# A sixth raw buffer, other planning numbers, and constants for the last bank's bits, in a two-layer hybrid attention kernel

## The chip, the cores and the metric

The kernel runs on one core of a Trainium2 chip. The metric is the time on the device in microseconds (us). Engines: PE (TensorE, matmuls; PEld its weight loads), DVE (VectorE), ACT (ScalarE), POOL (GpSimd), SP (which issues most DMAs).

## What is computed

Two layers over x (256 tokens, 1024 wide) and a memory mem of 256 tokens; `depth` is 2, heads are 64 wide.

```python
h = rms_norm(x, norm_g[layer]);  proj = h @ w_in[layer]          # 1024 x 3584
sb_q, sb_k, sb_v, sb_g, mb_q, mb_k, mb_v, mb_g, mem_q, mem_g = split(proj)
o_sb  = stick_breaking_attention(sb_q, sb_k, sb_v) * silu(sb_g)   # 6 heads
o_mb  = moba_attention(rope(mb_q), rope(mb_k), mb_v) * silu(mb_g) # 6 heads; here plain causal softmax
mk, mv = split(rms_norm(mem, mem_norm_g[layer]) @ w_mem_kv[layer])
o_mem = softmax_attention(mem_q, mk, mv) * silu(mem_g)            # 4 heads
x = x + concat(o_sb, o_mb, o_mem) @ w_out[layer]
# behind the last layer: rms_norm(x, final_norm_g)
```

Stick-breaking weights are exp(log sigmoid(z) + the sum over later keys of log(1 - sigmoid)).

## The kernel before

Every weight matrix is a **piece** (sb_qk, mb_q, mk, mv, ..., wo0 to wo2 for the output projection), loaded in **chunks** of 128 rows by 768 f32 values (384 KB) into a ring of `RAW` tiles, raw. ACT or DVE rounds a chunk to its **high part** (a cast, line 265 or 286) and DVE computes the **low part**, raw minus high (line 271); both lie in hl, a ring of seven. A product is three matmuls: high by high, high by low, low by high (the activations are split in the same way, into the tiles T, or mxhi and mxlo). The load of chunk j + RAW is issued by SP when the low part of chunk j has been queued:

```python
dma(raws[j % RAW]..., p.src[...], ("raw", j), q, now)      # dma_chunk
tt(los[j % LEAD], raws[j % RAW], his[j % LEAD], OP.subtract); dma_chunk(S.cur.t)   # lo_task
```

Nothing is ordered by hand beyond the lists `ORDER` (pieces by layer) and `KORD` (in which order the output projection takes its eight rows of 128). While the program is built, a list scheduler (`Sched`) plays all tasks against estimated engine times, DMA rates (`DMA_GBS`, `DMA_LAT`, ...), priorities (`PRI`, `P_*`) and slacks, and picks what each engine does next; the outcome is one fixed sequence for each engine, and on the chip each engine works its own off in order. So a number that only the scheduler reads changes the time through the sequence alone.

What the names in the rows are. Layer 0 works on h without the row factor of the norm; that factor, rbx, goes from DVE through a POOL DMA to DRAM and back to all partitions, and sb_q, sb_k and mem_q are multiplied by it on DVE. Score matmuls and value matmuls of a pair of heads use half the rows or columns of PE (`pair_scores`, form "row"; `pair_task`, form "col"); `HOLD` and `CROWD` say how long such a pair is held back to be bundled with others. For the softmax heads the weights are turned by a **trip**: DVE transposes 32-blocks into D, SP stores D to DRAM (Z) and loads it back turned in four DMAs (T<-Z; for rope ga or uT). The names in `HALVES` get eight DMAs instead. junk is a scratch tile: PE warms up on it, and ACT writes the squares of its row statistics there. In the last layer the last bank of wo2 is started by a matmul of no use, which sets the bank's bits (later it is overwritten by a copy of the residual, and the products accumulate on that).

Of the kernel before, what the change touches and what calls it, by code (L numbers as in the profile page):

```python
# [8 lines left out]
FR = mybir.dt.float32r  # L9
# [15 lines left out]
        "mb_q": (1536, 384), "mb_k": (1920, 384), "mb_v": (2304, 384), "mb_g": (2688, 384),  # L25
        "mem_q": (3072, 256), "mem_g": (3328, 256)}
LEAD = 7
RAW = 5
KORD = ((4, 5, 2, 3, 0, 1, 6, 7), (4, 5, 0, 1, 2, 3, 6, 7))
LAT_SAME, LAT_CROSS = 130.0, 240.0  # L30
PE_LATE = 173.4
NORM_LATE = 1845.2
DG_LATE = 816.9
COLD = 3900.0
PRI = {"sb": (54, 36), "mb": (6, 40), "mem": (44, 48)}
P_EV = 26
P_H0 = -8
P_RX = 2
P_M0 = 42
P_RM = 47  # L40
P_M1 = 50
URG = 2
X_AT = {5: 4, 6: 5, 7: 6, 8: 7}
CST_AT = 11
X0_AT = 9
X1_AT = 15
DMA_GBS = 355.0
SP_ISSUE = 450.0
POOL_ISSUE = 1000.0
POOL_TRIP = 5000.0  # L50
DMA_LAT = 2200.0
DMA_GBS_1K = 300.0
TRIP_LAT = 3500.0
MEM_AT = 1
ORDER = (["sb_qk", "mb_q", "mb_k", "mk", "mem_q", "mv", "sb_g", "sb_v", "mb_g", "mb_v", "mem_g"],
         ["mk", "mv", "mb_q", "mb_k", "sb_k", "sb_g", "mem_q", "sb_q", "sb_v", "mb_g", "mb_v", "mem_g"])
GATES = {"sb_g": ((0, 1), (2,)), "mb_g": ((0, 1), (2,)), "mem_g": ((0,), (1,))}
HOLD = 2000.0
HALVES = []
CROWD = 1  # L60
SPARE1 = 4
SPARE2 = 1
DVE_HI = 800.5
SLACK_PE = 26.0
SLACK = 104.7


def _free(ap):
    n = 1
    for d in ap.shape[1:]:  # L70
        n *= d
    return n
# [18 lines left out]
class Sched:  # L91
# [37 lines left out]
    def _avail(self, k, eng):  # L129
# [82 lines left out]
def hybrid_trunk(ctx: ExitStack, tc: tile.TileContext, x, mem, norm_g, w_in, w_mem_kv, w_out,  # L212
# [5 lines left out]
    S = Sched()  # L218
# [20 lines left out]
    def mm(out, lhsT, rhs, start, stop, **kw):  # L239
        n = _free(rhs)  # L240
        half = lhsT.shape[0] == 64 or out.shape[0] == 64
        if lhsT.dtype == FR:
            c = max(111.0, n * 0.4167 + (20.0 if n > 384 else 13.0))
        elif lhsT.dtype == BF:
            c = max(28.0, n * 0.44)
        else:
            c = max(110.0, n * 1.667 + 10.0)
        nc.tensor.matmul(out, lhsT=lhsT, rhs=rhs, start=start, stop=stop, **kw)  # L248
        m = (lhsT.shape[0], out.shape[0])
        c = (0.5 * c if half else c) + pe_mode(m, lhsT.dtype)  # L250
        S.op("pe", c * (1.8 if S.T["pe"] < COLD else 1.0))
# [41 lines left out]
    def sb(name, shape, dt=F32):  # L293
        return cpool.tile(shape, dt, name=name)
# [4 lines left out]
    gc = sb("gc", [128, 32])  # L299
    smask = sb("smask", [128, 128])  # L300
    cmask = sb("cmask", [128, 256])
    negT = sb("negT", [128, 128], FR)
    negone = sb("negone", [128, 128], FR)
    junk = sb("junk", [128, 512], BF)
    gb = sb("gb", [128, D])
    uT = sb("uT", [128, KT, 256])
# [14 lines left out]
    S.res["a"] = Res([sb(f"a{i}", [128, 384]) for i in range(3)])  # L321
    S.res["w"] = Res([sb(f"w{i}", [128, 512]) for i in range(4)])
    S.res["ah"] = Res([(sb(f"ah{i}", [128, 384], FR), sb(f"al{i}", [128, 384], FR)) for i in range(2)])
    S.res["wT"] = Res([sb(f"wT{i}", [128, 384]) for i in range(5)])
    S.res["D"] = Res([sb(f"D{i}", [128, 1024]) for i in range(2)])
    S.res["F0"], S.res["F1"] = Res([]), Res([])
    dpool = ctx.enter_context(tc.tile_pool(name="turn", bufs=1, space=bass.MemoryType.DRAM))
# [16 lines left out]
    dma_t = {"t": 500.0}  # L344

    def queue(nbytes, run, now):

        dma_t["t"] = max(dma_t["t"], now) + nbytes / (400.0 if run >= 3072 else DMA_GBS if run > 1024 else DMA_GBS_1K)
        return dma_t["t"] + DMA_LAT

    def dma(dst, src, name=None, q=None, now=0.0):
# [39 lines left out]
    for p in order:  # L391
        i = 0
# [13 lines left out]
    def dma_chunk(now=0.0, q=None):  # L406
        j = prog["dma"]
        if j >= len(chunks):
            return
        p, kk, c, w = chunks[j]  # L410
        n = len(kk)
        dma(raws[j % RAW][:, :n * w].rearrange("p (k c) -> p k c", c=w),
            p.src[:, kk[0]:kk[0] + n, c:c + w], ("raw", j), q, now)
        prog["dma"] += 1
        if j in X_AT:
            load_xT(X_AT[j], X_AT[j] + 1, now=now)
        for t, at in enumerate((X0_AT, X1_AT)):
            if j == at:
                dma(xs[:, t, :], x_r[:, t, :], ("x", t), now=now)
        if j == CST_AT:  # L420
            dma(cst, consts[:, 0:512], "cst", now=now)
            dma(S.res["w"].items[0][2][:, :256], consts[:, 512:768], "msk", now=now)

    def hi_task():
        for j, (p, kk, _, w) in enumerate(chunks):
            w = len(kk) * w
            e, _ = yield R(*([] if j in (0, 2) else [("act", 0.833 * w)]), ("dve", 0.52 * w + DVE_HI), 
                           need=[("raw", j)] + ([("free", j - LEAD)] if j >= LEAD else []))
            copy(his[j % LEAD][:, :w], raws[j % RAW][:, :w], e)
# [32 lines left out]
    load_xT(2, 3)  # L462
    dma_chunk()
    load_xT(3, 4)

    def bcast_row(vec, name):
        nc.gpsimd.dma_start(gb, bass.AP(tensor=vec.tensor, offset=vec.offset, ap=[[0, 128], [1, D]]))
        S.ready[name] = S.cur.t + 4000.0

    def setup():  # L470
        yield R("pool")
# [104 lines left out]
    def rows_done(key, name, rb):  # L576
        z = dpool.tile([1, 256], F32, name="rows_" + key)
        yield R("dve", need=["setup0", (key, "rows", 0), (key, "rows", 1)])
        nc.vector.transpose(rt, rcx if key == "x" else rcm)
        S.op("dve", 100.0)  # L580
        yield R("pool")
        for t in range(2):
            nc.gpsimd.dma_start(z[:, t * 128:t * 128 + 128].rearrange("o (i a) -> (o i) a", i=4), rt[t:128:32, :])
        S.op("pool", 2.0 * POOL_ISSUE)
        S.ready[name, "dump"] = S.cur.t + POOL_TRIP
        yield R("pool", need=[(name, "dump")])
        nc.gpsimd.dma_start(rb, z.broadcast_to([128, 256]))
        S.op("pool", POOL_ISSUE)
        S.ready[name] = S.cur.t + POOL_TRIP

    def rows_task(l, src, key, name, rc, rb):
        for t in range(2):
# [3 lines left out]
    def norm_task(l, t, H, done):  # L596
# [423 lines left out]
    def main():  # L1020
# [26 lines left out]
        for l in range(DEPTH):  # L1047
# [15 lines left out]
            def T_piece(n, X, nchunk, need, post):  # L1063
                p = pieces[n, l]
                for c in range(nchunk):
                    acc = yield from bank()
                    yield from tr_unit(p, X, c, acc, need, c == nchunk - 1)
                    S.spawn(post(c, acc), P_EV, S.cur.t)

            def N_piece(n, X, need, post):  # L1070
                p = pieces[n, l]
                for t in range(2):
                    acc = yield from bank()
                    yield from nat_unit(p, X, t, acc if n == "mv" else acc[:, :p.width], need)
                    S.spawn(post(t, acc), P_EV, S.cur.t)

# [5 lines left out]
            for h in range(SBH):  # L1082
                S.spawn(sb_head(l, h), PRI["sb"][1] + h)
            for h in range(MEMH):
                S.spawn(soft_head(l, h, "mem"), PRI["mem"][1] + h)
            for h in range(SBH):
                S.spawn(soft_head(l, h, "mb"), PRI["mb"][1] + h)
            for kind, n in (("sb", 3), ("mb", 3), ("mem", 2)):
                for c in range(n):
                    S.spawn(pair_scores(l, kind, c), PRI[kind][0] + 2)  # L1090
                    S.spawn(pair_sums(l, c) if kind == "sb" else pair_turn(l, kind, c), PRI[kind][0] + 1)
                    S.spawn(pair_task(l, kind, c), PRI[kind][0])
            if l == 0:
                p = pieces["sb_qk", 0]
                accs = []
# [70 lines left out]
            accs = {}  # L1166
            for i, k0, k1 in ((0, 0, 6), (1, 0, 6), (0, 6, 8), (1, 6, 8), (2, 0, 8)):
                p = pieces[f"wo{i}", l]
                w = p.width
                for t in range(2):  # L1170
                    if k0 == 0 and (i, t) not in accs:
                        accs[i, t] = yield from bank()
                    if (l, i, t) == (1, 2, 0):
                        accs[2, 1] = yield from bank()
                        mm(accs[2, 1][:, :256], junk[:, :128], junk[:, :256], True, True)
                        S.spawn(seed_task(accs[2, 1]), 0, S.cur.t)
                    yield from nat_unit(p, X, t, accs[i, t][:, :w], xneed, k0, k1, (l, i, t) == (1, 2, 1))
                    if k1 == KT:
                        S.spawn(resid_task(l, i, t, accs[i, t], w, hN), 0, S.cur.t)
# [58 lines left out]
```

## Time and profile before

| | |
|---|---|
| three timed runs | 275.11, 278.11, 277.42 us; median 277.42 |
| the profiled execution | 277.1 us, of which the span of the instructions is 275.2 |
| busy | PE 96%, PEld 87%, DVE 83%, ACT 70%, POOL 3% of the span |
| granted PE clock | 0.994 |
| moved | 62.34 MB, 226 GB/s |
| chain that ended last | PE 84%, DVE 9%, DMA 2%, ACT 1% |

A row of the timeline has the start, the length, the engine, the line, the operation, out<-in, shape and count; in brackets the idle time before it and what ended it. Neighbouring instructions of a kind are merged, and since matmuls are pipelined the distance of two starts says more than a length.

### The profile page before, as it was taken

To read this page: it belongs to the slowest core of one execution; us is meant where nothing else is said; L and a number is where in the kernel's file an instruction comes from. 1 tells how busy PE (TensorE), PEld (TensorE's weight loads), DVE (VectorE), ACT (ScalarE), POOL (GpSimd) and SP (SyncE) were. 2 spreads that over 40 slices of the span, in tenths; PEclk is the share of its full clock that TensorE was granted. 3 is DMA by queue.
4 is the path that set the end of the run, shared out by engine and by line. 5 is a ranking of instruction groups with operands and counts; after the bars stand their busy time and mean duration, and the time that the engine had idled before them with its cause. 6 is when DMAs were issued, how large, how long until landed. Compare 5 with 4: busy or idle time off the path is not lost.

```text
span 275.2 us, 4955 instructions
## 1 busy us (share of the span) xinstructions
PE 265.4 (96%) x1653; PEld 239.1 (87%) x1653; DVE 229.6 (83%) x543; ACT 193.0 (70%) x441; POOL 7.6 (3%) x19
## 2 busy tenths in 40 slices
PE   8999997999999999999999999999999999999992
PEld 5889995897997898898988999888889889898991
DVE  3797996999999999995889778649999999979082
ACT  3787994998888596770886545559699689675053
POOL 0002100002000000000000000000000000000000
PEclk9999999999999999999999999999999999999997
DMA  6999989986977789684487866777348876972004
GB/s 213 338 399 369 347 237 316 296 260 180 296 229 210 231 259 272 232 200 152 132 248 250 288 225 225 232 225 204 89 163 245 260 242 182 341 231 88 0 2 152
DMA packets 47593, 62.34 MB, mean 226 GB/s; under 512 B 3728, under 2 KB 44048, under 8 KB 47568
## 3 DMA queue, kind: packets, MB, share of 16 engines
q1 hardware_dynamic: 46480, 59.93, 69.1%
q0 software_dynamic: 512, 1.31, 1.7%
q10 hardware_dynamic: 576, 0.79, 0.8%
q8 instruction: 13, 0.21, 0.3%
q14 instruction: 12, 0.10, 0.1%
HBM read 54.94 MB, written 7.08 MB: 225 GB/s over the span
## 4 chain that ended last, share of the span: by engine, by line
PE 84%; DVE 9%; DMA 2%; issue 1%; ACT 1%; DVEq 0%
PE bank L248 84%; DVE hl L271 3%; DMA raw<-in_w_mem_kv_dram 2%; DVE al L271 1%; DVE bank L271 1%; PE bank L254 1%; DVE xs L271 1%; DVE mem_q L275 0%; ACT junk L267 0%; ACT hl L265 0%; DVE a L275 0%; DVE ah L286 0%; DVE sb_k L275 0%; DVE sb_q L275 0%; DVE mv L275 0%
## 5 line engine op out<-in xcount | busy, mean ns | idle before, releaser
L271 DVE TENSOR_TENSOR hl<-raw,hl 128x768 fp32r<-128x768 f32 (+3 forms) x114 | 101.4, 899 | 11.7 <-ACT hl L265 10.5
L248 PE MATMUL bank<-T,hl 128*128 128x512 f32 (+1 forms) x582 | 107.1, 340 | 0.6 <-DVE st L740 0.6
L248 PEld LDWEIGHTS bank<-T,hl 128*128 128x128 f32 x582 | 89.2, 190 | 14.6 <-issue 1.7
L265 ACT CAST hl<-raw 128x768 fp32r<-128x768 f32 (+2 forms) x111 | 87.4, 796 | 15.2 <-PE bank L248 4.4
L248 PE MATMUL bank<-hl,T 128*128 128x384 f32 (+1 forms) x448 | 80.3, 336 | 0.0
L248 PEld LDWEIGHTS bank<-hl,T 128*128 128x128 f32 x448 | 76.7, 188 | 1.8 <-issue 0.3
L248 PE MATMUL bank<-hl,mxhi 128*128 128x384 f32 (+1 forms) x192 | 45.2, 319 | 0.0
L248 PEld LDWEIGHTS bank<-hl,mxhi 128*128 128x128 f32 x192 | 33.3, 189 | 0.8 <-issue 0.8
L248 PE MATMUL bank<-hl,mxlo 128*128 128x384 f32 (+1 forms) x96 | 30.4, 317 | 0.0
L267 ACT ACTIVATE junk<-xs 128x384 bf16<-128x384 f32 (+2 forms) x15 | 8.0, 537 | 20.8 <-DVE xs L271 20.3
L248 PEld LDWEIGHTS bank<-hl,mxlo 128*128 128x128 f32 x96 | 18.1, 189 | 0.1
L267 ACT ACTIVATE ga<-ga 128x256 f32<-128x256 f32 (+1 forms) x36 | 17.4, 488 | 0.9 <-DVE ga L275 0.7
L267 ACT ACTIVATE T<-uT,gc 128x256 fp32r<-128x256 f32 x24 | 11.8, 502 | 3.9 <-DMA uT<-xT_dram 3.9
L265 ACT COPY gT<-bank 128x256 f32<-128x256 f32 x16 | 5.9, 370 | 11.6 <-PE bank L248 11.4
L271 DVE TENSOR_TENSOR xs<-bank,xs 128x384 f32<-128x384 f32 (+1 forms) x11 | 5.7, 520 | 8.7 <-PE bank L248 8.7
L267 ACT ACTIVATE a<-a 128x384 f32<-128x384 f32 x24 | 12.4, 533 | 0.0
L783 DVE STREAM_TRANSPOSE D<-w 128x384 f32<-128x384 f32 (+1 forms) x20 | 12.4, 623 | 0.0
L275 DVE SCALAR_TENSOR_TENSOR T<-uT,gc,T 128x256 fp32r<-128x256 f32 x24 | 11.4, 480 | 1.1 <-ACT T L267 1.1
L279 DVE TENSOR_SCALAR w<-w,st 128x256 f32<-128x256 f32 (+1 forms) x40 | 11.3, 327 | 0.0
L267 ACT ACTIVATE w<-w,st 128x128 f32<-128x128 f32 (+1 forms) x24 | 10.6, 446 | 0.7 <-DVE st L740 0.5
L271 DVE TENSOR_TENSOR gT<-bank,gT 128x256 f32<-128x256 f32 x16 | 6.7, 417 | 4.1 <-ACT gT L265 4.1
L267 ACT ACTIVATE w<-bank,st 128x256 f32<-128x256 f32 x16 | 7.4, 474 | 2.4 <-DVE st L753 2.4
(114 smaller groups left out, 261.4 us busy)
## 6 DMA issues: line engine op xcount, KB each, us to landing
raw<-in_w_in_dram SPq DMA_DIRECT2D x70, 384.0 KB, 4.5
raw<-in_w_out_dram SPq DMA_DIRECT2D x17, 384.0 KB, 4.6
Z<-D SPq DMA_DIRECT2D x10, 384.0 KB, 4.2
raw<-in_w_mem_kv_dram SPq DMA_DIRECT2D x8, 384.0 KB, 5.4
T<-Z SPq DMA_DIRECT2D x24, 96.0 KB, 4.3
uT<-memT_dram SPq DMA_DIRECT2D x8, 256.0 KB, 6.5
Z<-D SPq DMA_DIRECT2D x4, 512.0 KB, 4.5
T<-Z SPq DMA_DIRECT2D x16, 128.0 KB, 4.8
```

The lines of the kernel that those rows point to most:

```text
L248: nc.tensor.matmul(out, lhsT=lhsT, rhs=rhs, start=start, stop=stop, **kw)
L254: nc.tensor.transpose(out, in_, idt)
L265: nc.scalar.copy(out, in_)
L267: nc.scalar.activation(out, in_, func, **kw)
L271: nc.vector.tensor_tensor(out, a, b, op=op)
L275: nc.vector.scalar_tensor_tensor(out, a, s, b, op0=op0, op1=op1)
L279: nc.vector.tensor_scalar(out, a, s, None, op0=op)
L783: nc.vector.transpose(o, w[:, :n * 128].rearrange("p (m j r) -> p m j r", j=4, r=32))
```

## The change

RAW goes from 5 to 6, with a load more ahead of the first instruction; to make room, the wT ring goes from 5 to 4 tiles. The scheduler's DMA rates are lower, and the two broadcasts of rows go through its queue model. Its priorities, slacks, ORDER, KORD, HOLD and SPARE2 have other values, and five trips are in HALVES. negT and negone become one tile, neg, and the matmul that sets the last bank's bits reads neg instead of junk.

```diff
-RAW = 5
-KORD = ((4, 5, 2, 3, 0, 1, 6, 7), (4, 5, 0, 1, 2, 3, 6, 7))
+RAW = 6
+KORD = ((0, 1, 2, 3, 4, 5, 6, 7), (2, 3, 0, 1, 4, 5, 6, 7))
...
-DMA_GBS = 355.0
+DMA_GBS = 330.0
...
-MEM_AT = 1
-ORDER = (["sb_qk", "mb_q", "mb_k", "mk", "mem_q", "mv", "sb_g", "sb_v", "mb_g", "mb_v", "mem_g"],
+MEM_AT = 0
+ORDER = (["sb_qk", "mb_q", "mb_k", "mem_q", "mv", "sb_g", "mk", "sb_v", "mb_v", "mb_g", "mem_g"],
...
-HOLD = 2000.0
-HALVES = []
+HOLD = 10878.7
+HALVES = [("F", 1, "mb", 1), ("F", 0, "mem", 1), ("F", 1, "mem", 1), ("F", 1, "mb", 2), ("F", 0, "mem", 0)]
...
-    negT = sb("negT", [128, 128], FR)
-    negone = sb("negone", [128, 128], FR)
+    neg = sb("neg", [128, 256], FR)
+    negT, negone = neg[:, 0:128], neg[:, 128:256]
...
-    S.res["wT"] = Res([sb(f"wT{i}", [128, 384]) for i in range(5)])
+    S.res["wT"] = Res([sb(f"wT{i}", [128, 384]) for i in range(4)])
...
+    for _ in range(RAW - 5):
+        dma_chunk()
...
-                        mm(accs[2, 1][:, :256], junk[:, :128], junk[:, :256], True, True)
+                        mm(accs[2, 1][:, :256], negone, neg, True, True)
```

What this makes of the sequences is shown at three places. First PE, layer 0, at the first scores of the stick-breaking heads (out sb_q, sb_k). Before, T_74 holds the tokens and T_75 the memory; in the change T_73 holds the tokens and T_74 the memory. Eight matmuls of mem_q stand between the last of mk and the scores before:

```order
L248 MATMUL bank_105<-T_75,hl_100 128x512
L248 MATMUL bank_106<-T_74,hl_94 128x512
L248 MATMUL bank_106<-T_74,hl_94 128x256
L248 MATMUL bank_106<-T_74,hl_94 128x512
L248 MATMUL bank_106<-T_74,hl_94 128x256
L248 MATMUL bank_106<-T_74,hl_94 128x512
L248 MATMUL bank_106<-T_74,hl_94 128x256
L248 MATMUL bank_106<-T_74,hl_95 128x512
L248 MATMUL bank_106<-T_74,hl_95 128x256
L248 MATMUL bank_108<-sb_q,sb_k 128x256
```

Now, with all of mem_q and nearly all of mv ahead of them (the last rows of the 60):

```order
L248 MATMUL bank_106<-hl_94,T_74 128x512
L248 MATMUL bank_106<-hl_94,T_74 128x256
L248 MATMUL bank_106<-hl_95,T_74 128x512
L248 MATMUL bank_106<-hl_95,T_74 128x256
L248 MATMUL bank_106<-hl_95,T_74 128x512
L248 MATMUL bank_106<-hl_95,T_74 128x256
L248 MATMUL bank_107<-sb_q,sb_k 128x256
```

The scores stand 20 matmuls later behind mb_k than they did. Second DVE at the same place, down to the products that the scores need. The rows hl<-raw are low parts. Before:

```order
L271 TENSOR_TENSOR rn_136<-rn_136,cst 128x6x16
L271 TENSOR_TENSOR rn_136<-rn_136,ru_137 128x6x16
L898 STREAM_TRANSPOSE D_126<-rn_136 128x3x4x32
L271 TENSOR_TENSOR hl_97<-raw_93,hl_97 128x768
L275 SCALAR_TENSOR_TENSOR mem_k<-bank_104,mem_k 128x256
L275 SCALAR_TENSOR_TENSOR sb_q<-sb_q,rbx 128x256 x3
L275 SCALAR_TENSOR_TENSOR sb_k<-sb_k,rbx 128x256 x3
```

Now:

```order
L901 STREAM_TRANSPOSE D_125<-rn_135 128x3x4x32
L271 TENSOR_TENSOR hl_96<-raw_93,hl_96 128x512
L271 TENSOR_TENSOR hl_97<-raw_88,hl_97 128x768
L275 SCALAR_TENSOR_TENSOR mem_q<-bank_108,mem_q 128x256
L271 TENSOR_TENSOR hl_98<-raw_89,hl_98 128x768
L551 TENSOR_SCALAR ss_157<-ss_157 128x1
L275 SCALAR_TENSOR_TENSOR sb_q<-sb_q,rbx 128x256 x3
L275 SCALAR_TENSOR_TENSOR sb_k<-sb_k,rbx 128x256 x3
```

hl_97 holds chunk 24 in both; it belongs to mv before and to sb_g now, and chunk 25 (hl_98) now stands ahead of sb_q too. Third SP, at the end of layer 0, where the trips of the memory heads (Z, then T) stand among the loads of the output projection. Before:

```order
L928 DMA T_75<-Z_131 32x4x256 x4
L352 DMA raw_89<-in_w_out_dram 128x2x384
L352 DMA raw_90<-in_w_out_dram 128x2x384
L917 DMA Z_129<-D_125 128x1024
L352 DMA raw_91<-in_w_out_dram 128x2x384
L352 DMA raw_92<-in_w_out_dram 128x2x384
L352 DMA raw_93<-in_w_out_dram 128x2x256
L352 DMA raw_89<-in_w_out_dram 128x2x256
L928 DMA T_75<-Z_129 32x4x256 x4
```

Now:

```order
L920 DMA Z_128<-D_124 128x1024
L352 DMA raw_91<-in_w_out_dram 128x2x384
L352 DMA raw_92<-in_w_out_dram 128x2x384
L931 DMA T_74<-Z_130 32x2x256 x8
L352 DMA raw_93<-in_w_out_dram 128x2x384
L352 DMA raw_88<-in_w_out_dram 128x3x256
L931 DMA T_74<-Z_128 32x2x256 x8
```

Both trips come back in eight smaller DMAs; two loads stand between the two trips' loads now, where two loads, a store and four loads stood.

More of the change, by code (lines that the diff above doesn't have):

```diff
@@ L27 @@
 LEAD = 7
-RAW = 5
-KORD = ((4, 5, 2, 3, 0, 1, 6, 7), (4, 5, 0, 1, 2, 3, 6, 7))
+RAW = 6
+KORD = ((0, 1, 2, 3, 4, 5, 6, 7), (2, 3, 0, 1, 4, 5, 6, 7))
 LAT_SAME, LAT_CROSS = 130.0, 240.0
-PE_LATE = 173.4
-NORM_LATE = 1845.2
-DG_LATE = 816.9
+PE_LATE = 303.1
+NORM_LATE = 361.3
+DG_LATE = 226.3
 COLD = 3900.0
-PRI = {"sb": (54, 36), "mb": (6, 40), "mem": (44, 48)}
-P_EV = 26
+PRI = {"sb": (58, 36), "mb": (18, 36), "mem": (48, 52)}
+P_EV = 23
 P_H0 = -8
[L38 to L41, printed above, removed]
+P_RX = -3
+P_M0 = 27
+P_RM = 37
+P_M1 = 60
 URG = 2
@@ L44 @@
 CST_AT = 11
-X0_AT = 9
+X0_AT = 11
 X1_AT = 15
-DMA_GBS = 355.0
+DMA_GBS = 330.0
 SP_ISSUE = 450.0
 POOL_ISSUE = 1000.0
-POOL_TRIP = 5000.0
+POOL_TRIP = 5500.0
 DMA_LAT = 2200.0
-DMA_GBS_1K = 300.0
+DMA_GBS_1K = 285.0
 TRIP_LAT = 3500.0
-MEM_AT = 1
-ORDER = (["sb_qk", "mb_q", "mb_k", "mk", "mem_q", "mv", "sb_g", "sb_v", "mb_g", "mb_v", "mem_g"],
-         ["mk", "mv", "mb_q", "mb_k", "sb_k", "sb_g", "mem_q", "sb_q", "sb_v", "mb_g", "mb_v", "mem_g"])
+MEM_AT = 0
+ORDER = (["sb_qk", "mb_q", "mb_k", "mem_q", "mv", "sb_g", "mk", "sb_v", "mb_v", "mb_g", "mem_g"],
+         ["mv", "mk", "mb_q", "mb_k", "sb_k", "sb_g", "mem_q", "sb_q", "sb_v", "mb_g", "mb_v", "mem_g"])
 GATES = {"sb_g": ((0, 1), (2,)), "mb_g": ((0, 1), (2,)), "mem_g": ((0,), (1,))}
-HOLD = 2000.0
-HALVES = []
+HOLD = 10878.7
+HALVES = [("F", 1, "mb", 1), ("F", 0, "mem", 1), ("F", 1, "mem", 1), ("F", 1, "mb", 2), ("F", 0, "mem", 0)]
 CROWD = 1
 SPARE1 = 4
[L62 to L65, printed above, removed]
+SPARE2 = 2
+DVE_HI = 647.3
+SLACK_PE = 0.0
+SLACK = 104.6
 def _free(ap):
@@ L346, in queue @@
     def queue(nbytes, run, now):
-        dma_t["t"] = max(dma_t["t"], now) + nbytes / (400.0 if run >= 3072 else DMA_GBS if run > 1024 else DMA_GBS_1K)
+        dma_t["t"] = max(dma_t["t"], now) + nbytes / (380.0 if run >= 3072 else DMA_GBS if run > 1024 else DMA_GBS_1K)
         return dma_t["t"] + DMA_LAT
@@ L464, in hybrid_trunk @@
     load_xT(3, 4)
+    for _ in range(RAW - 5):
+        dma_chunk()
     def bcast_row(vec, name):
         nc.gpsimd.dma_start(gb, bass.AP(tensor=vec.tensor, offset=vec.offset, ap=[[0, 128], [1, D]]))
-        S.ready[name] = S.cur.t + 4000.0
+        S.ready[name] = queue(524288, 4096, S.cur.t + 2400.0) + 1000.0
     def setup():
@@ L588, in rows_done @@
         S.op("pool", POOL_ISSUE)
-        S.ready[name] = S.cur.t + POOL_TRIP
+        queue(400000, 4096, S.cur.t)
+        S.ready[name] = S.cur.t + POOL_TRIP + 1500.0
     def rows_task(l, src, key, name, rc, rb):
```

## The prediction

> **What bounds the kernel now.** I read the busy table first, then the list of who waited for whom, then the timeline around the longest wait, then the stretches.
>
> ```profile
> PE 265.4 (96%) x1653; PEld 239.1 (87%) x1653; DVE 229.6 (83%) x543; ACT 193.0 (70%) x441; POOL 7.6 (3%) x19
> PE bank L248 <- DVE sb_k L275: 2.4, 1, 2.4
> PE bank L248 <- DVE junk L1023: 1.2, 1, 1.2
> PE bank L248 <- DVE st L740: 0.6, 1, 0.6
> PE bank L248 <- ACT junk L267: 0.3, 1, 0.3
> ```
>
> TensorE (PE) is busy for 96% of the span, and the four rows of waits are all it ever waits: 2.4 for the scaled sb_k, 0.6 for a softmax statistic, 0.3 for the scratch tile junk, and 1.2 at the start. Nothing else stands between its matmuls but the cost of changing their form. So this change can win what lies in three rows, 3.3 us and a little more, by removing waits; every other gain would need cheaper matmuls, and there the order is permuted, not shortened. Now the longest wait.
>
> ```profile
> 38.97 7.16 PE L248 MATMUL bank<-T,hl 128*128 128x512 f32 x40
> 48.49 2.23 PE L248 MATMUL bank<-sb_q,sb_k 64*128 64x256 f32 x24 [2.37 <-DVE sb_k L275]
> 38.34 1.02 SPq L352 DMA_DIRECT2D raw<-in_w_mem_kv_dram  x2
> 44.94 0.84 ACT L265 CAST hl<-raw 128x768 fp32r<-128x768 f32 x1 [4.18 <-DMA raw<-in_w_mem_kv_dram]
> 45.80 0.96 DVE L271 TENSOR_TENSOR hl<-raw,hl 128x768 fp32r<-128x768 f32 x1 [2.61 <-ACT hl L265]
> 47.10 1.00 DVE sb_q L275 x3
> 48.10 1.01 DVE sb_k L275 x3
> 54.97 2.63 PE L248 MATMUL bank<-hl,T 128*128 128x512 f32 x14
> ```
>
> Read backwards (columns: start, length, engine, line, what; in brackets the idle time before it and who ended it). The first score matmuls of the stick-breaking heads start at 48.49, after 2.37 of idling. They wait for sb_k, which DVE scales by rbx only after sb_q. DVE gets there late since, in its fixed order, it first computes the low part of a weight chunk of mv; that waits for ACT's high part, and that waits until 44.94 for the chunk, issued from 38.34 on: 6.6 us. The first matmul of mv stands at 54.97, ten us later (last row): the chunk is looked ahead for, and the engine that looks ahead is blocked.
>
> ```profile
> 48.50:120.80 72.30, 71.74 (x461) 63.23 (x462) 70.54 (x185) 60.87 (x148) 2.25 (x4) 1.00 0.82 245
> 132.40:260.00 127.60, 127.60 (x807) 116.13 (x806) 105.40 (x238) 86.62 (x192) 0.54 (x1) 1.00 0.67 209
> ```
>
> The stretches (busy PE, PEld, DVE, ACT, POOL, then clock, DMA share, GB/s): from the scores to wo1, the second piece of layer 0's output projection, PE has 71.74 of 72.30 and DVE 70.54, 97.6%: two engines bound this stretch. In layer 1 PE is full and DVE has 22 us to spare. The granted clock is 1.00 in both.
>
> **The scores of layer 0.** In the new order, between mb_k and the scores, stand the 32 matmuls of mem_q and 28 of mv, where 32 of mk and 8 of mem_q stood: 20 more. The first row quoted above has 40 matmuls from 38.97 to 46.13, 0.18 each; 20 take 3.5 to 3.6. PE then reaches the scores at 46.1 + 3.5 = 49.6 without waiting, later than sb_k was there even before (48.49). On DVE two low parts (chunks 24 and 25) and a piece of mem_q stand ahead of sb_q instead of one low part and a piece of mk. If chunk 24 landed no earlier, at 44.94, DVE would start the first low part at 45.8 and need 0.87 + 0.34 + 0.87 + 0.1 + 1.0 (three sb_q) + 0.4 (one sb_k) = 3.6: ready at 49.4, just in time.
>
> ```profile
> 57.43 0.87 DVE hl L271
> 46.76 0.34 DVE mem_k L275
> 35.48 0.92 DVE L271 TENSOR_TENSOR hl<-raw,hl 128x768 fp32r<-128x768 f32 x1
> 36.94 0.95 DVE L271 TENSOR_TENSOR hl<-raw,hl 128x768 fp32r<-128x768 f32 x1
> 37.79 0.58 POOL L587 DMA_DIRECT2D rbx<-rows_x  x1 [4.49 <-DMA rows_x<-rt]
> rbx<-rows_x POOLq DMA_DIRECT2D x1, 128.0 KB, 6.1
> ```
>
> With six raw buffers chunk 24 is issued after the low part of chunk 18, not 19: in the rows above two such low parts in a row end at 36.4 and 37.9, and the new order puts a few small pieces more ahead of the earlier one, so I count the issue about 1 us earlier and sb_k ready at 48.4 to 49.4. The bounds of this edit: nothing won (the chunk lands over 0.3 later than now) to 2.4 won. I take the **2.4**. rbx comes over POOL: issued at 37.79 and 6.1 under way, it was there at about 44; the transposed statistics that start this chain keep their place in DVE's order, so it is no rival for last place.
>
> **What DVE then allows.** I added up the instructions that the order has between the scores and wo1, each by the mean distance of starts of its shape in the trace: on PE 68.7 before and 65.4 now, on DVE 70.1 (the window shows 70.54) and 68.3. PE's 68.7 becomes the 72.3 of the window by seven changes of form (0.27 each, below, 1.9), the wait of 0.6 for st, and 1.1 that I cannot name and carry on. Now it is 65.4, ten changes (2.7) and 1.1: 69.2. DVE at its 97.6% needs 70.0. From 49.6 the stretch ends at 118.8 by PE and at 119.6 by DVE, not at 120.8: 1.2 to 2.0 earlier, all of the wait at sb_k and st and the added visits being in it. I take **1.7**: DVE idled there in part because it waited for PE, so the PE end is the nearer.
>
> **More visits to the half-array.** Score and value matmuls use 64 rows or columns. I count 14 stretches of them before (8 in layer 0, 6 in layer 1) and 17 now (11 and 6).
>
> ```profile
> 87.42 1.52 PE L248 MATMUL bank<-wT,sb_v 128*64 128x256 f32 x16
> 88.87 0.62 PE L248 MATMUL bank<-T,hl 128*128 128x512 f32 x2
> 89.42 0.87 PE L248 MATMUL bank<-wT,sb_v 128*64 128x256 f32 x8
> 90.22 0.98 PE L248 MATMUL bank<-T,hl 128*128 128x512 f32 x4
> PEld bank L248 <- issue: 5.6, 22, 0.4
> ```
>
> Two pairs in one visit take 88.87 - 87.42 = 1.45. From 88.87 to 90.22 is 1.35 for two ordinary matmuls (0.36) and one pair (0.73), so a visit by itself costs 0.27, and three cost 0.8, which is in the stretch above. The last row is the same thing on the weight loads, 0.25 each time. The Trainium skill, TensorEngine Tiling (Array Packing), section Key Properties, says that changing the tiling mode drains the engine. Were the drain as long as a whole matmul (0.34 in a row below) at both ends, a visit would cost 0.7, three 2.0, and the sum would be 276.2 by that rule; the 0.27 of the rows speaks for much less.
>
> **The seed of the last bank.** Before wo2 of layer 1 a matmul of junk by junk sets the bank's bits.
>
> ```profile
> 263.78 0.10 PEld L248 LDWEIGHTS <-junk 128*128 128x128 bf16 x1 [0.63 <-ACT junk L267]
> 263.78 0.28 PE L248 MATMUL bank<-junk 128*128 128x256 bf16 x1 [0.32 <-ACT junk L267]
> 262.61 0.51 PE L248 MATMUL bank<-hl,mxhi 128*128 128x384 f32 x2
> 263.13 0.34 PE L248 MATMUL bank<-hl,mxhi 128*128 128x384 f32 x1
> 263.78 6.04 PE bank L248 x49
> ```
>
> junk is also where ACT's squares go, so PE waits for ACT. From 262.61 to 263.13 stand three matmuls (two of mxhi, one of mxlo between), 0.17 each; from 263.13 to 263.78 one, so 0.48 is lost. The constants neg are written once, in the first 25 us. Their matmul is in the weights' type and costs at most the 0.17 of a wider one: 0.3 to 0.5 won, I take **0.4**. If the bank or the chunk of wo2 came last instead, nothing; but the low parts for wo2 stand earlier in the new order. Behind the last matmul (263.78 + 6.04) stay 5.4 us of residual, norm and output, the same as now.
>
> **Cheap or covered edits.**
>
> ```profile
> L286 DVE CAST hl<-raw 128x768 fp32r<-128x768 f32 x1 | 0.6, 560 | 0.2 <-DMA raw<-in_w_in_dram 0.2
> L267 ACT ACTIVATE wT<-bank 128x384 f32<-128x384 f32 x12 | 5.4, 500 | 0.0
> 137.96 0.75 DVE L275 SCALAR_TENSOR_TENSOR w<-xs,ss,gb 128x512 f32<-128x512 f32 x1 [1.19 <-ACT ss L267]
> 140.99 0.38 PE L254 MATMUL bank<-cst,w 128*128 128x128 f32 x2
> ```
>
> The lower rates, priorities and KORD act through the order alone. MEM_AT 1 to 0 changes nothing: that turn of the loop has no work of its own for sb_qk. DVE takes two more 768-wide casts (0.56 each, 1.1) and ACT fewer; that is in the counts. One wT buffer less: 0 while four do, up to one exponential (0.50) otherwise. The norm's first transposes follow wo2 by 8 matmuls, not 16, 1.4 earlier: at 139.6 where they stood at 140.99; their operand was ready at 138.7, so 0.9 is left: 0, and at most 0.5 where the next ones are closer. The sixth buffer draws one load into the first us, where PE's list of waits has no chunk: 0. Value pairs that follow their sums by some 1.2 us, while ACT needs two exponentials (1.0), are tight; 0 to 0.3, and I take 0.
>
> **Halved trips.** Five turned weights now come back in eight transfers each, not four.
>
> ```profile
> 116.21 1.84 SPq L928 DMA_DIRECT2D T<-Z  x4
> 126.09 1.08 PE L248 MATMUL bank<-T,mv 128*64 128x256 f32 x8
> T<-Z SPq DMA_DIRECT2D x16, 128.0 KB, 4.8
> T<-Z SPq DMA_DIRECT2D x24, 96.0 KB, 4.3
> ```
>
> Four issues take 1.84, eight 3.7. Before, the last trip of layer 0 was issued by 118.05, landed by 122.9 and was used at 126.09: 3.2 to spare. Now the issue ends 1.9 later and the use stands nine matmuls (1.6) earlier: at the edge, but the issue also stands some places earlier among the weight loads. I cost it at 0, with 0 to 1.9 for each of the two trips of layer 0; in layer 1 the last pair is moved 27 matmuls (4.7 us) later, which covers it. Smaller transfers could land sooner, up to the difference of the two rows above, 0.5, which nobody waits for. The Trainium skill, DMA: Bandwidth & Descriptors, section Rules for kernel authors, tells one to coalesce, and calls transfers under 64 KB mostly overhead. These become 48 and 64 KB, and by that rule the third rival comes true; no run shows such a halved trip yet.
>
> **Sum.** The profiled execution took 277.1, its span of 275.2 and 1.9 around it; the three timed runs have a median of 277.42, 0.3 above. 277.1 - 1.7 - 0.4 = **275.0**, 0.9% below the median. About 1% is what a measurement of this kernel can tell from no change (its runs lie from 275.11 to 278.11).
>
> **Rivals.** (1) *More is won* (0.18): PE runs through the stretch without the 1.1 that I could not name, and without new waits: 275.0 - 0.3 - 1.1 = 273.6. For it: DVE has 1.8 less to do there, and its low parts come later than now. (2) *The wait stays* (0.15): chunk 24 or 25 lands a us or more later than now, since one more load is queued ahead of it, and DVE hands that on to sb_k. Then only st and the seed are won and the visits paid: 277.1 + 0.8 - 0.6 - 0.4 = 276.9. This is also what comes if the sixth buffer doesn't do what it is there for, the load being held by those in front of it on SP. (3) *Trips late* (0.09): eight issues hold up weight loads, or land late: 1.9 at each of two trips, 275.0 + 3.8 = 278.8. (4) *DVE is the bound, and it gets slower than before* (0.12): the two moved casts (1.1) fall into DVE's full stretch, and PE, early at the scores, waits at the sums and softmaxes instead: 277.1 + 1.1 + 0.8 = 279.0, and 280.9 with one late trip. It decides once DVE's work from scores to wo1 is over 72.
>
> **How the numbers follow.** The forecast has 0.46, its own range 274.2 to 276.2 (the ends of DVE and PE, the norm, the tight pairs). The range 273.2 to 279.2 reaches to all rivals and leaves out the ends of (1), (3) and (4), under 0.2. Faster by over 1% is below 274.65: 0.20 of the forecast's 0.46 and all of (1), 0.38. Slower by over 1% is above 280.2, where (3) and (4) come together or one is dearer than priced: half of (4) and a third of (3), 0.09. The rest is within 1%: 0.53.
>
> **What would show it.** In the waits of PE, sb_k is gone or under 0.5, ACT junk is gone, and nothing over 1 us is new. ACT's wait for the raw chunk before 45 is under 3. The stretch from the first scores to wo1 takes 69 to 70. If sb_k still has over 1.5, it is (2); a wait for T<-Z, (3); several waits for DVE between 50 and 120, (4). I am wrong altogether if the layer 1 stretch, full now, shows new waits.

## The result, and the profile after

The changed kernel takes **274.62 us** (median of nine runs, 274.0 to 275.1), the kernel before, run beside it, 277.48 (275.11 to 280.07): ratio 0.9915, 95% interval 0.9885 to 0.9944. The ratio goes by the means of the runs within 1.5% of the fastest of their kernel, which leaves out the three longest of the nine of before. The forecast was 275.0. The profiled execution took 275.1, its span 273.3. First the busy table and the list of PE's waits (engine, line, waited for: us in total, times, longest) of the changed kernel:

```profile
PE 266.9 (98%) x1653; PEld 239.0 (87%) x1653; DVE 231.5 (85%) x545; ACT 191.6 (70%) x437; POOL 6.9 (3%) x19
PE bank L248 <- DVE junk L1026: 1.2, 1, 1.2
```

Only the wait of the first microsecond is left; sb_k, st and ACT's junk are gone. Then the timeline around the first scores of layer 0 (start, length, engine, line, what; in brackets the idle time and who ended it):

```profile
38.00 1.47 SPq L352 DMA_DIRECT2D raw<-in_w_in_dram  x2
43.64 0.84 ACT L265 CAST hl<-raw 128x768 fp32r<-128x768 f32 x1 [0.66 <-DMA raw<-in_w_in_dram]
46.57 0.96 DVE L271 TENSOR_TENSOR hl<-raw,hl 128x768 fp32r<-128x768 f32 x1 [0.31 <-ACT hl L265]
48.51 1.09 DVE L275 SCALAR_TENSOR_TENSOR sb_k<-sb_k,rbx 128x256 f32<-128x256 f32 x3
45.23 5.10 PE L248 MATMUL bank<-hl,T 128*128 128x512 f32 x28
50.26 2.01 PE L248 MATMUL bank<-sb_q,sb_k 64*128 64x256 f32 x20
```

Chunk 24 is issued at 38.00 and rounded at 43.64 (38.34 and 44.94 before); ACT waits for it 0.66, not 4.18. The last sb_k is ready at 49.60, 0.7 ahead of PE, which comes to the scores behind 28 matmuls of mv. The stretches (busy PE, PEld, DVE, ACT, POOL, then clock, DMA share, GB/s):

```profile
39.64:50.26 10.62, 10.62 (x61) 9.06 (x61) 9.56 (x24) 7.66 (x17) 0.54 (x1) 1.00 1.01 331
50.26:119.57 69.31, 69.31 (x442) 59.70 (x441) 67.72 (x175) 57.66 (x142) 1.70 (x3) 1.00 0.80 238
150.10:262.10 112.00, 112.00 (x698) 101.81 (x696) 91.26 (x218) 73.04 (x166) 0.00 (x0) 1.00 0.66 195
```

PE is full in all three. Set against the same places of before:

| stretch of PE | before | after | difference | forecast |
|---|---|---|---|---|
| start to the end of mb_k | 38.97 | 39.64 | +0.67 | 0 |
| to the first scores | 9.52 | 10.62 | +1.10 | with the next |
| scores to wo1 of layer 0 | 72.30 | 69.31 | -2.99 | both: -1.7 (measured -1.89) |
| wo1 to mb_q of layer 1 | 30.39 | 30.53 | +0.14 | 0 |
| mb_q to the seed of the last bank | 112.60 | 112.00 | -0.60 | -0.4 |
| seed to the end | 11.46 | 11.20 | -0.26 | 0 |
| span | 275.2 | 273.3 | -1.9 | -2.1 |

The seed, in the timeline of the changed kernel, then its two halved trips of layer 0 on SP with the rows of its DMA list (KB each, us to landing):

```profile
261.92 0.33 PE L248 MATMUL bank<-hl,mxhi 128*128 128x384 f32 x1
262.10 0.28 PE L248 MATMUL bank<-neg 128*128 128x256 f32 x1
262.21 0.28 PE L248 MATMUL bank<-hl,mxhi 128*128 128x256 f32 x1
```
```profile
106.89 4.88 SPq L931 DMA_DIRECT2D T<-Z  x8
112.87 5.44 SPq L931 DMA_DIRECT2D T<-Z  x8
```
```profile
T<-Z SPq DMA_DIRECT2D x24, 64.0 KB, 3.4
T<-Z SPq DMA_DIRECT2D x16, 48.0 KB, 3.1
```

The seed costs 0.11 and waits for nothing. Eight issues take 4.9 and 5.4 us, not the 3.7 that I had reckoned, but no wait for T stands in PE's list.

### The profile page after: what moved, and what is told of

Its sections match the earlier page's. It is cut to its first block, busy times and chain, and to the rows that moved or that the text cites. A ratio compares the mean times of both kernels' runs of the same rounds, so it can differ in the third digit from the quotient of the medians.

```text
span 273.3 us, 4987 instructions
## 1 busy us (share of the span) xinstructions
PE 266.9 (98%) x1653; PEld 239.0 (87%) x1653; DVE 231.5 (85%) x545; ACT 191.6 (70%) x437; POOL 6.9 (3%) x19
## 4 chain that ended last, share of the span: by engine, by line
PE 98%; ACT 0%; DVE 0%; DVEq 0%; issue 0%
PE bank L248 97%; PE bank L254 1%; ACT ss L267 0%; ACT junk L267 0%; DVE xs L279 0%; DVEq L1237 0%; DVE junk L1026 0%
## 5 line engine op out<-in xcount | busy, mean ns | idle before, releaser
L265 ACT CAST hl<-raw 128x768 fp32r<-128x768 f32 (+3 forms) x107 | 84.9, 805 | 12.4 <-PE bank L248 5.1
L248 PE MATMUL bank<-hl,T 128*128 128x384 f32 (+1 forms) x448 | 82.0, 338 | 0.0
L267 ACT ACTIVATE T<-uT,gc 128x256 fp32r<-128x256 f32 x24 | 11.1, 502 | 3.9 <-DMA uT<-xT_dram 3.9
L271 DVE TENSOR_TENSOR ev<-bank,gT 128x256 f32<-128x256 f32 x16 | 6.5, 419 | 5.1 <-PE bank L248 5.1
L271 DVE TENSOR_TENSOR mxlo<-ev,mxhi 128x256 fp32r<-128x256 f32 x16 | 6.6, 418 | 2.3 <-ACT mxhi L265 2.2
```

The costliest lines, as they stand in the source:

```text
L265: nc.scalar.copy(out, in_)
L267: nc.scalar.activation(out, in_, func, **kw)
L271: nc.vector.tensor_tensor(out, a, b, op=op)
```

## The experiments

Most of them keep a sequence fixed: the scheduler's picks are written out as a list and taken in that order, so that only the named thing differs. "Numbers" are the values that the scheduler reads. Each ratio is to the kernel before, run beside it; its median lay between 276.35 and 278.01 from one experiment to the next.

**1. The seed alone, and the wait in two more executions.**

```diff
 before:
-    negT = sb("negT", [128, 128], FR); negone = sb("negone", [128, 128], FR)
+    neg = sb("neg", [128, 256], FR); negT, negone = neg[:, 0:128], neg[:, 128:256]
-    mm(accs[2, 1][:, :256], junk[:, :128], junk[:, :256], True, True)
+    mm(accs[2, 1][:, :256], negone, neg, True, True)
```

> The kernel before with one edit: neg in place of negT and negone, and the last bank's bits set by neg instead of junk; every engine's sequence stays what it was. By the theory (PE waits there for ACT's squares in junk) the wait for ACT junk goes from the list of PE, the distance from the last matmul of 384 columns to the first of wo2 falls from 0.65 us to 0.28 or less, and the span by 0.4 to 0.5, from 275.2 to 274.7 or 274.8. A rival: the bank or the chunk of wo2 comes last there, and the wait only changes its name (0).

PE's wait, then the timeline of this run:

```profile
PE bank L248 <- DVE sb_k L275: 0.3, 1, 0.3
```
```profile
43.33 0.83 ACT L265 CAST hl<-raw 128x768 fp32r<-128x768 f32 x1 [2.31 <-DMA raw<-in_w_mem_kv_dram]
44.19 0.96 DVE L271 TENSOR_TENSOR hl<-raw,hl 128x768 fp32r<-128x768 f32 x1 [1.12 <-ACT hl L265]
46.88 2.23 PE L248 MATMUL bank<-sb_q,sb_k 64*128 64x256 f32 x24 [0.28 <-DVE sb_k L275]
261.66 0.33 PE L248 MATMUL bank<-hl,mxhi 128*128 128x384 f32 x1
261.84 0.28 PE L248 MATMUL bank<-neg 128*128 128x256 f32 x1
```

From the last wide matmul to the seed it is 0.18 (0.65 before): 0.47 won, as forecast. But the span of this one execution is 273.3, 1.9 less, and the rest comes from a place that this edit doesn't touch: with the same sequence up to there, **the wait for sb_k is 0.28, not 2.37**, since chunk 24 was there 1.6 us earlier and PE came to the scores 0.5 later (at 46.60, not 46.12). So a third execution, of the kernel before with nothing changed but the picks written out:

> The kernel before once more, its sequence written out, for a third look at the wait for sb_k. If the landing of chunk 24 varies from one execution to the next, the wait lies between 0.2 and 2.5 us and the span follows it, 273.8 with the shortest and 275.3 with the longest, and DVE's low part of chunk 24 starts as much later as the wait is longer. If the wait is a fixed part of this sequence, it is 2.2 to 2.5.

Its timeline at the scores, and its stretches behind them:

```profile
45.54 0.96 DVE L282 TENSOR_TENSOR hl<-raw,hl 128x768 fp32r<-128x768 f32 x1 [1.85 <-ACT hl L276]
48.22 3.48 PE L259 MATMUL bank<-sb_q,sb_k 64*128 64x256 f32 x24 [2.54 <-DVE sb_k L286]
```
```profile
48.00:50.00 2.00, 1.78 (x15) 1.57 (x17) 2.00 (x6) 1.83 (x4) 0.00 (x0) 0.75 0.97 330
50.00:52.00 2.00, 2.00 (x13) 1.61 (x12) 1.71 (x6) 1.93 (x7) 0.55 (x1) 0.50 0.99 296
52.00:54.00 2.00, 2.00 (x11) 1.71 (x11) 1.95 (x4) 0.88 (x4) 0.00 (x0) 0.89 0.76 245
```

Wait 2.54, span 276.3, time 278.08: longer than the wait explains. The number behind the POOL column is PE's granted clock. After this wait it is at 0.5 for 3.4 us, the 24 score matmuls take 3.41 us (to 51.63) instead of 2.16, and the 24 of mem_q behind them 4.65 instead of 4.31. The wait thus varies from 0.3 to 2.5 in three executions of one sequence, and in this one it cost 1.6 more. My upper bound on the span (275.3) left that out. My other expectation failed too: the low part of chunk 24 starts at 45.54, 0.26 earlier than where the wait was 2.37. The wait is the distance of two things that both move: ACT took up chunk 24 at 43.33, 44.67 and 44.94, and PE came to the scores at 46.60, 45.68 and 46.12 (waits 0.28, 2.54, 2.37).

**2. What stands behind the wait.** The kernel before with five buffers, its sequence kept but for the steps that I thought blocked sb_k; DVE's row of steps (ACT's high parts 24 and 25 moved with it):

```diff
 DVE: ... D<-rn
-  lo 24
   mem_k, sb_q x3, sb_k x3
+  lo 24
   mem_k, sum of gb's squares, lo 25, masks of the scores
```

> The kernel before, its sequence written out, with three steps moved: ACT's high parts of chunks 24 and 25 and DVE's low part of chunk 24 stand behind the six products of sb_q and sb_k with rbx, not ahead of them. By the theory (the look-ahead at chunk 24 blocks DVE, and through it sb_k) PE's wait of 2.4 us is under 0.3 and the scores start at 46.1 to 46.5 instead of 48.49; DVE uses the 2.6 us in which it idled, so that 1.7 to 2.4 of it last to the end: 272.8 to 273.5 as span. A rival: the stretch after it is bound by DVE or by the chunks of mv, which now come later on DVE, and under 1 us lasts (over 274.2), with new waits of PE for low parts or sums. A second rival: rbx itself comes late, and PE waits for sb_k nevertheless, 1 us or more.

In its timeline:

```profile
46.75 0.63 ACT L278 ACTIVATE junk<-gb 128x512 bf16<-128x512 f32 x1 [4.75 <-DMA gb<-in_mem_dram]
48.50 0.96 DVE L282 TENSOR_TENSOR hl<-raw,hl 128x768 fp32r<-128x768 f32 x1 [2.91 <-ACT hl L276]
54.56 2.69 PE L259 MATMUL bank<-hl,T 128*128 128x512 f32 x14 [1.61 <-DVE mem_q L286]
```

The scores start at 45.74 without a wait, and nothing of it lasts: 277.75 against 276.36 of the kernel before beside it, ratio 1.0043 (1.0012 to 1.0075). ACT now sits 4.75 us at the squares of the second half of the memory's rows, whose load (gb) lands as late as the chunks; the high parts stand behind it, DVE idles 2.91, and PE waits for mem_q. So that too was moved out of the way, behind lo 25:

> The kernel before with five raw buffers, its sequence written out, with five steps moved: as in the run with sb_q and sb_k first, and besides ACT's squares of the second half of the memory's rows (junk<-gb) and the sum behind them on DVE stand behind the low part of chunk 25. The theory now: at this place three transfers land late in turn (chunk 24, chunk 25, the memory's rows in gb), and each blocks ACT and DVE, which work in order; the run that moved two of them idled at the third. With all three moved PE waits neither for sb_k nor for mem_q, DVE's masks of the scores start at 48.0 to 48.9 instead of 50.28, and 1.4 to 2.2 us last: 274.5 to 275.5 as time where the kernel before has a median of 276.4. The rival: DVE's work itself bounds the stretch, whatever it waits for: time within 0.5 of the kernel before, and new waits of PE at the sums or softmaxes.

Its timeline, and a stretch behind:

```profile
48.21 0.62 ACT L276 CAST hl<-raw 128x512 fp32r<-128x512 f32 x1 [1.19 <-DMA raw<-in_w_mem_kv_dram]
50.39 0.84 ACT L276 CAST hl<-raw 128x768 fp32r<-128x768 f32 x1 [1.56 <-DMA raw<-in_w_in_dram]
55.89 4.19 PE L259 MATMUL bank<-hl,T 128*128 128x512 f32 x14 [3.17 <-DVE mem_q L286]
```
```profile
58.00:60.00 2.00, 2.00 (x8) 1.71 (x8) 2.00 (x5) 2.00 (x5) 0.00 (x0) 0.50 1.00 296
```

277.46 against 276.35, ratio 1.0035 (1.0007 to 1.0064): wrong again. ACT now reaches chunks 26 and 27 before they land, the squares come behind them at 51.13, DVE's sum and then its masks wait for the squares, and PE idles 3.17; the clock falls here too. Both theories that named a culprit fell. With five buffers what blocks the engines is not one step but all that is loaded from 38 to 42: both orders, which brought PE to the scores at 46, met the next late load.

**3. The ring alone.** The sequence of before, with six buffers:

```diff
-RAW = 5
+RAW = 6          # and wT from 5 to 4, one load more ahead
```

> The kernel before, its sequence written out and kept, with six raw buffers and four for wT; one exponential of a stick-breaking head, which needs a fifth wT, stands later on ACT, ahead of nothing that PE waits for by the trace. By the theory (chunk 24 is issued one low part earlier) it lands 0.8 to 1.5 us earlier, and PE's wait for sb_k falls from 2.4 to between 0.9 and 1.6: span 273.7 to 274.6. A rival: the DMA engines are full there and the chunk lands when it did, wait 2.4 and span 275.2. Another: the exponential that is moved costs what is won.

The timeline of this run:

```profile
45.26 0.83 ACT L276 CAST hl<-raw 128x768 fp32r<-128x768 f32 x1 [2.88 <-DMA raw<-in_w_mem_kv_dram]
46.12 2.23 PE L259 MATMUL bank<-sb_q,sb_k 64*128 64x256 f32 x24
47.09 0.63 ACT L278 ACTIVATE junk<-gb 128x512 bf16<-128x512 f32 x1 [0.99 <-DMA gb<-in_mem_dram]
53.30 2.74 PE L259 MATMUL bank<-hl,T 128*128 128x512 f32 x14 [0.55 <-DVE mem_q L286]
```

Chunk 24 is issued at 36.12, 2.2 earlier than before, is in time, and PE's wait for sb_k is gone, more than I expected, but the time is 276.72 against 276.36, ratio 1.0013 (0.9993 to 1.0032). ACT stops at chunk 25 and at gb instead. Of the 2.37 won at the scores 1.67 are left at mv and 0.55 at the value matmuls of the stick-breaking heads; there the exponential that I had to move takes 0.56, against my expectation. Left to itself with six buffers and the old numbers, the scheduler makes another sequence:

> The kernel before with six raw buffers, four for wT and one load more ahead, and the scheduler left to make its own sequence of it with the old numbers; the first scores stand 254 matmuls in, two later than before. The theory (the ring by itself only hands the wait on, to the memory's rows and the next chunks, since PE reaches the scores at the same place) gives a time within 0.7 of the kernel before (275.7 to 277.1), and a narrower spread of the runs, under 1.6 us where five buffers show over 3. The rival, a sequence made for six buffers wins by the ring alone: 275.3 or less.

In its timeline, at the scores and at the output projection of layer 0:

```profile
46.41 2.23 PE L248 MATMUL bank<-sb_q,sb_k 64*128 64x256 f32 x24
107.06 5.52 SPq L352 DMA_DIRECT2D raw<-in_w_out_dram  x4
112.63 3.78 SPq L930 DMA_DIRECT2D T<-Z  x8
117.47 1.55 PE L248 MATMUL bank<-T,mb_v 128*64 128x256 f32 x8 [5.58 <-DMA T<-Z]
```

284.6, ratio 1.0268 (1.021 to 1.0327). The theory that the ring only hands the wait on does not hold here: PE comes to the scores at 46.41, as early as before, and has no wait over 0.3 from the first microsecond to the output projection (mv starts at 52.56, 2.4 earlier). Then two trips stand on SP behind four loads that take 5.5 us to issue: PE waits 5.58, then 1.10, and the clock falls to 0.5. The spread was the narrow one expected, 1.4. The miss is in my expectation of the time, which went by the first 60 us alone.

**4. The numbers alone.** The sequence of after with five buffers, first with the halved trips, then with whole ones (`RAW = 5`, wT still at four; then also `HALVES = []`):

> The changed kernel, its sequence written out and kept, with five raw buffers and without the sixth early load. By the theory (the new order moves the scores 3.5 us back, the sixth buffer brings each chunk about 1 us earlier, and sb_k is there 0.6 us before PE) a wait of 0.3 to 1.0 us for sb_k comes back, with a few small ones for chunks elsewhere: span 273.6 to 274.8. A rival, the order alone does it: 273.3 and no wait. The other rival, the buffer does it: the wait is over 1.5 us and the span over 275.

Two of its rows, each with a wait of PE:

```profile
52.33 2.23 PE L259 MATMUL bank<-sb_q,sb_k 64*128 64x256 f32 x24 [0.76 <-DVE sb_k L286]
132.11 0.44 PE L259 MATMUL bank<-hl,mxhi 128*128 128x384 f32 x1 [1.22 <-ACT mxhi L276]
```

280.55, ratio 1.0152 (1.0108 to 1.0196), the whole range missed: sb_k waits 0.76 as expected, but other places lose as well: 2.1 of the 7.6 us of span come up to the scores, 2.4 from the start of wo0 to wo2 of layer 0 (112.2 to 131.5 in the changed kernel), 2.0 late in layer 1.

> The changed kernel, its sequence written out and kept, with five raw buffers and with whole trips. With five buffers and halved trips the time was 280.55, 5.9 above the changed kernel, of which 2.4 came between the trips at the end of layer 0 and the end of wo1 (118.5 to 131.4 in the changed kernel) and 2.1 at the first scores. If the eight issues on SP are what the sixth buffer has to hide there, whole trips give back those 2.4 or a good part: 277.8 to 279. If the ring alone is short, the time stays within 0.7 of 280.5.

281.5, ratio 1.0172 (1.0134 to 1.021). From the start of wo0 to wo2 1.2 is lost, not 2.4. From 118.5 on alone, the place as I named it, it had been 1.9 and is nothing; 1.3 are lost just ahead of it instead. The wait for sb_k is 1.12, and the total is no better. The ring is short by itself. The scheduler, told of five buffers, finds nothing better with the new numbers:

> The changed kernel with five raw buffers, and the scheduler left to make its own sequence of it with the new numbers; the first scores then stand 256 matmuls in, not 272, and there are 21 visits to the half-array, not 17. The theory (new numbers and sixth buffer belong together): slower than the kernel before or equal, 276.4 to 279, with PE waiting for sb_k or for chunks, 1 us for the four visits, and a spread over 2.5 us. The rival, the numbers do it: 275.3 or less.

280.37, ratio 1.011 (1.0053 to 1.0167): PE waits 0.7 for sb_k, 2.3 in four places for low parts and 0.9 for a high part.

**5. The old order of the pieces, all else new.**

```diff
-MEM_AT = 0
-ORDER = (["sb_qk", "mb_q", "mb_k", "mem_q", "mv", "sb_g", "mk", "sb_v", "mb_v", "mb_g", "mem_g"],
+MEM_AT = 1
+ORDER = (["sb_qk", "mb_q", "mb_k", "mk", "mem_q", "mv", "sb_g", "sb_v", "mb_g", "mb_v", "mem_g"],
```

> The changed kernel with the old order of layer 0's pieces (mk ahead of mem_q and mv); all other numbers and the ring of six are the new ones. The scheduler still puts the first scores 272 matmuls in, 20 later than before, now behind mk and 28 matmuls of mem_q. If the place of the scores with six buffers is what counts, not which pieces stand ahead of them, there is no wait for sb_k and the time is within 0.8 of the changed kernel's 274.6. If mv ahead of the scores is needed (its chunks being those that are looked ahead for), the wait is back with over 1 us: 275.6 or more.

The scores, and the longest wait, in its timeline:

```profile
49.75 2.23 PE L248 MATMUL bank<-sb_q,sb_k 64*128 64x256 f32 x24
116.94 0.69 PE L248 MATMUL bank<-hl,mxhi 128*128 128x384 f32 x1 [3.94 <-ACT mxhi L265]
```

There is no wait at the scores, whichever piece fills the room; the time, expected within 0.8 of 274.6, is missed. It is 283.74, ratio 1.0242 (1.0181 to 1.0302): 3.94 of waiting at wo0 for a gated output and a half clock behind it, then 0.8 each for another output and for a trip. PE began wo0 at 111.77, 0.4 ahead of the changed kernel. So scores without a wait are not enough; what this sequence loses, it loses at the end of layer 0.

**6. Terms that were costed at little.** The changed kernel, its sequence kept, with whole trips (`HALVES = []`):

> The changed kernel, its sequence written out and kept, with all turned weights loaded back in four transfers each instead of eight for five of them. By the prediction's costing the halves are neither paid for nor of use while six buffers hold: time within 0.3 us of the changed kernel's 274.6, no wait of PE over 0.3. A rival, eight issues hold up the loads behind them on SP: whole trips are 0.5 to 2 us faster (below 274.1). The other rival, the halves land sooner and PE needs that: 0.5 us or more slower, with a wait for T<-Z.

274.52 (274.1 to 275.11), ratio to before 0.9936 (0.9912 to 0.996), PE's list of waits the same single row. The halves neither cost nor bring anything. The Trainium skill, DMA: Bandwidth & Descriptors, section Rules for kernel authors, calls transfers under 64 KB mostly overhead; of these transfers that means the ones of 48 KB, and no price for them shows here: those of 48 and of 64 KB land in 3.1 and 3.4 us and hide. Then two visits fewer:

```diff
 PE:  value matmuls of sb pairs 1, 2
+     scores of mem pair 1
      six matmuls of mb_v
-     scores of mem pair 1
 ...
-     value matmuls of mb pair 0
      28 matmuls of mb_g
+     value matmuls of mb pair 0
      value matmuls of mb pair 1
```

> The changed kernel, its sequence written out, with two steps of PE moved: the scores of the second pair of memory heads follow the value matmuls of the stick-breaking heads at once (six matmuls earlier), and the first rope pair's value matmuls stand right ahead of the second's (ten matmuls of mb_g and 28 more later). Visits to the half-array fall from 17 to 15. By the prediction's price of 0.27 us for one, 0.5 is won: span 272.8 against 273.3, time 274.1 against 274.6, without new waits. A rival, by which a visit costs the drain of a whole matmul at both ends (0.7): 1.4 won. The other: the later outputs make PE wait at the output projection, nothing won or worse.

The changed kernel's rows first, then those of this run, from the timeline, and two of its waits:

```profile
87.09 1.52 PE L248 MATMUL bank<-wT,sb_v 128*64 128x256 f32 x16
95.15 1.90 PE L248 MATMUL bank<-T,hl 128*128 128x512 f32 x10
```
```profile
86.09 1.52 PE L259 MATMUL bank<-wT,sb_v 128*64 128x256 f32 x16
93.92 1.78 PE L259 MATMUL bank<-T,hl 128*128 128x512 f32 x9
```
```profile
PE bank L259 <- DVE hl L282: 0.3, 1, 0.3
PE bank L259 <- DVE mxlo L282: 0.2, 1, 0.2
```

The same 54 matmuls up to the last row take 8.06 with two visits and 7.83 with one: 0.23 for a visit. The second move brings new waits, and the time is 274.76, the same as the changed kernel's. No version was faster than that by more than the noise.

## Why the prediction was right, by its steps

**The scores.** PE came to them 10.62 behind the end of mb_k, as reckoned (49.6 - 38.97 = 10.63), and sb_k was there in time. Less the 0.67 that the start of this execution took, chunk 24 was issued 1.0 earlier than before, as counted, and sb_k was ready at 48.9 (reckoned: 48.4 to 49.4). What failed in this step is the wait as a fixed 2.4: it is one draw from 0.3 to 2.5, and sometimes a half clock comes with it. That the forecast hit is in part luck, since it was made against an execution of 277.1, close to the median of the runs beside it. Against the execution of experiment 1, less the seed's share, the change would have looked worth 0.5 in span. The sum was lucky too: the start cost 0.67 that it did not have, and its other terms together won 0.5 more than it gave them.

**Where the gain comes from.** I gave the sixth buffer a microsecond and the place of the scores the rest. For the time, the runs show neither alone: six buffers in the old sequence 1.0013, the new sequence with five 1.0152, both 0.9915. For the wait at the scores they show the shares the other way round. It is gone in all six traces with six buffers, whether PE comes to the scores at 46 (experiment 3, both runs) or at 50; with five it stays, at 0.76 and 1.12, though the scores stand late (experiment 4). What the new sequence does beside that is to keep the end of layer 0 free, where two other sequences with six buffers lose 5.58 and 3.94 at one wait (experiments 3 and 5). And it needs the sixth buffer at six more places (3.3 of waiting in all with five). The size of this (5.9 us without it) is nowhere in the prediction.

**Scores to wo1.** Forecast 69.2 by PE, measured 69.31, the 1.1 that I couldn't name included. Rival (1) is out. The mechanism of rival (4), in which PE is early and waits in mem_q and the sums, is what experiments 2 and 3 ran into; in the new sequence it does not occur.

**The seed** (0.4): 0.47, shown by itself. **A visit** (0.27): 0.23. The Trainium skill, TensorEngine Tiling (Array Packing), section Key Properties, says that a change of tiling mode drains the engine, and gives no length. The length that I tried, a whole matmul at both ends or 0.7, would have put the sum at 276.2 and is not borne out. **Trips** (0): 0, by the run with whole ones, though the issues took 4.9 to 5.4 and not 3.7. **Norm and tight pairs** (0): no wait in layer 1.

**Not in the sum:** the first 39 us, +0.67. That is no work of the change, as the last section shows.

**Open:** which of the new numbers (rates, priorities, KORD) make the end of layer 0 fit; why the loads land when they do; and what experiment 3's sequence would win without the moved exponential.

## What to carry to other kernels

A wait on a load, read from one profiled execution, is a sample: read it in a second and a third before pricing its removal. Where several loads come due together and the engines work in order, taking one blocked step away uncovers the next; here a deeper ring took the wait away, and moving its consumer back alone did not. A list scheduler's sequence and the buffers it was made for are one thing: changed one at a time, each looked useless or worse here.

## What the hardware showed besides

**A wait can halve PE's clock, and where it falls decides.** Granted 0.5 came behind idle times of 2.54, 3.17, 3.94 and 5.58 (experiments 1, 2, 5, 3) and not behind 1.61 and 2.37. The traces' record of the granted clock tells more. It falls only at whole multiples of 3.41 us behind the moment at which it first rose to full, and stays low for 3.41, 3.41, 6.83 and 10.24 us. Cut into such stretches of 3.41, all fourteen traces, the idle time behind the last matmul included, agree: each stretch in which PE was idle for 2.02 us or more ends with the clock at 0.5, and none with 1.86 or less makes it fall. The wait of 2.37 lay across an edge, 0.7 on one side and 1.7 on the other; that of 2.54 lay within one stretch, and the clock fell 0.8 us after PE had gone on. That it is the idle time in a stretch that counts is read off these cases; no run tested it. The Trainium skill, TensorE: Matmul & The Clock Gate, section Part 1: The HAM clock gate, tells of a clock that halves after an idle window of about 3.4 us, which runs free of the kernel; the traces agree on the window, but it need not be idle throughout.

**The same clock at the start is a matter of luck.** The first rows are the kernel before, the next the changed one, the last the third execution of experiment 1; between the two rows of each stand the same 102 matmuls.

```profile
4.87 17.60 PE L248 MATMUL bank<-T,hl 128*128 128x256 f32 x102
22.30 0.87 PE L248 MATMUL bank<-hl,T 128*128 128x384 f32 x4
```
```profile
5.08 17.34 PE L248 MATMUL bank<-T,hl 128*128 128x256 f32 x98
22.97 0.33 PE L248 MATMUL bank<-hl,T 128*128 128x384 f32 x1
```
```profile
4.76 17.27 PE L259 MATMUL bank<-T,hl 128*128 128x256 f32 x102
21.87 0.52 PE L259 MATMUL bank<-hl,T 128*128 128x384 f32 x2
```

17.43, 17.89 and 17.11. In the traces the first of them follow each other at 0.21 and later at 0.12; the step comes at 5.9 before, at 7.0 after, and at 4.6, ahead of them all, where the start is fastest. At these moments the record of the granted clock begins; the clock column has 1.00 ahead of it too, where there is no record. In the fourteen traces the record begins between 4.0 and 7.1, with both sequences. The seed-only run, with the old sequence, needed 17.92, and experiment 6, with the new one, reached the second row at 22.72 and 21.97. So up to 0.8 us of span is drawn anew each time.

**With six buffers the times of a kernel spread less.** Two sequences were run with both depths. The old one lay from 274.9 to 278.5 with five buffers (23 runs) and from 276.4 to 277.6 with six (12 runs); the new one from 279.3 to 282.7 with five (6 runs) and from 274.0 to 275.1 with six (9 runs). The others with nine runs or more agree (over 3 us with five, within 1.5 with six). Those with four runs do not: 0.9 and 2.2 with five, 1.4 and 2.9 with six. Why it is so is open.
